# Layer 1 of a two-layer encoder: score units of a bank issued together, values with tokens on partitions for four heads, and splits on 128 rows laid out by DMA

## The chip, the cores and the metric

The kernel runs on one core of one Trainium2 chip. Its time is the device time of one execution in microseconds (us), and less is better. TensorE (PE) multiplies matrices out of SBUF into PSUM, VectorE (DVE), ScalarE (ACT) and GpSimd (POOL) work element by element, and SyncE (SP) issues most transfers. Each engine takes its instructions in order.

## The reference

A two-layer encoder over 512 tokens (an 8 x 64 grid) of width 1024, all in float32. Layer 0 has two head groups (grouped-query attention and latent attention) and is not touched but for one flag. Layer 1, which the change is about, is neighbourhood attention with 16 heads of 64:

```python
q, k, v = split(h @ w_qkv, 3)                       # 512 x 1024 each, 16 heads of 64
for each query: window of 8 rows x 16 columns       # all 8 rows of the grid, 16 columns
    sc = q . k[window] * 64**-0.5 + bias[head, row difference, column difference]
    o  = softmax(sc) . v[window]
h = h + o @ w_out
```

Each layer is followed by a squared-ReLU MLP of width 4096, and a final norm ends the whole.

## The kernel before

**Two halves of a number.** Every product is computed from numbers split into a high and a low part (`hi`, `lo`, a copy rounded by ScalarE and the rest by VectorE), as three matmuls: hi x hi, hi x lo, lo x hi. Lines 426 to 428 (`mm3`) are these three for the dense products, with the weights stationary and 512 tokens moving, so that outputs have their features on partitions. Weights come in chunks by `plan` and `weights` (two chunks ahead of their use, four `raw` buffers), are split into `whi` (L192, ScalarE) and `wlo` (L193, VectorE), and a product walks over its chunks.

**The attention of layer 1.** Tokens stand column by column of the grid (8 rows together), so that a block of 128 queries needs a band of 256 keys: a *unit*. A head has four units, u = 0 to 3, the last one for both ends of the sequence. For each unit, `unit` (L1207) issues two matmuls of 256 columns (L1217), which take the query's halves on the 128 rows of the contraction (64 features high, 64 low) against the key's high and low part. VectorE adds the bias and takes the minimum (L1221), ScalarE does the exponential (L1223), VectorE the reciprocal (L1224), GpSimd the normalisation (L1225). Two units share one PSUM bank `s` (there are two such banks): `scores` (L1228) calls `unit` for u = 3 and 0, then for 1 and 2, so the matmuls of a unit stand between the two halves' vector work in the program. The probabilities are transposed by TensorE (L1236, four 128 x 128 blocks for each of T1 and T2), split into halves (L1240 ScalarE, L1241 VectorE), and multiplied with the values in `finish` (eight matmuls, L1251), whose two halves are added (L1262, L1263).

**Projections.** `projC(t)` computes Q, K and V of the two heads 2t and 2t+1 at once: three column tiles of 128 in three `mm` banks, 8 k-tiles each, 72 matmuls of 512 columns. Its evacuation `ev` normalises (`hold["rb"]`, the reciprocal root of the norm, broadcast over partitions) and splits:

```python
                    for e in range(2):
                        a, z = 64 * e, 64 * (1 - e)
                        # Q: hi of head e on 64 rows, lo on the other 64     (L1177 ACT, L1178 DVE)
                        # K: hi and lo of head e on 64 rows, copied to the other 64
                        #                      (L1183 ACT, L1184 DVE, one DMA of GpSimd's queue, L1186)
```

So Q and K take two ScalarE and two VectorE instructions each, on 64 rows. V is normalised (L1189), transposed by TensorE in four blocks (L1192) to get tokens on partitions, and split (L1196, L1197).

**What sets the order.** The order of the instructions on each engine is fixed when the program is built, by a scheduler that takes the next instruction that its own timing has ready, in the order of the program otherwise. In the program, the attention of a head is written in three steps, and after each step `fill.run(us)` takes so many microseconds' worth of matmuls out of a queue of other products: first `projC(1)` to `projC(7)` (head 2t begins with `fill.until` of projection t), and from head 13 on the output projection of the first six head pairs. `projC(0)` runs ahead of the attention, with the sum of squares of the tokens (`rows_r1`: L446, a chain of small VectorE instructions, four transposes L454).

## Time and profile before

| what | value |
|---|---|
| runs shown | 1220.49, 1221.71, 1222.97 us; median 1221.71 |
| profiled execution | 1220.6 us, its span 1218.8 us |
| granted TensorE clock | 0.997 |
| TensorE matmuls busy | 1189.6 us (98%) |
| VectorE, ScalarE, GpSimd busy | 814.0, 628.3, 411.5 us |
| layer 1's projection ahead of the attention | begins at about 617 us |
| first and last score matmul of layer 1 | 641.3 and 840.6 us |

The span runs from the first to the last instruction that the profiler saw. A row of a group names line, engine, operation, output and inputs, shapes and count, then busy time and mean duration of one, then the idle time of the engine ahead of these instructions and what ended it. A row of the timeline gives the start, the duration (first start to last end where several are merged), and the instruction. A matmul's duration holds the way through the array, so matmuls of a stream overlap in their records.

### The profile page before, as it was taken

How to read it: one execution, taken by the hardware profiler on the slowest of the kernel's cores; microseconds unless marked ns; L12 is line 12 of the kernel's file. 1: busy time of each engine (PE TensorE's matmuls, PEld its weight loads, DVE VectorE, ACT ScalarE, POOL GpSimd, SP SyncE). 2: the span in 40 equal slices, each digit the busy share in tenths (PEclk: the TensorE clock that was granted, in tenths of full speed). 3: DMA queues.
4: the chain of work that ended last, by engine and by line, in shares of the span. 5: the costliest groups of instructions: out<-in, count | busy, mean ns of one | idle time of the engine just before them, and what ended most of it. 6: DMA issues, size and time to landing. Idle time of an engine off the chain costs nothing.

```text
span 1218.8 us, 18461 instructions
## 1 busy us (share of the span) xinstructions
PE 1189.6 (98%) x6644; PEld 1003.4 (82%) x6644; DVE 814.0 (67%) x1433; ACT 628.3 (52%) x1051; POOL 411.5 (34%) x535
## 2 busy tenths in 40 slices
PE   9998999999999999999999999999999999999997
PEld 8676788887899889898877777778788988988985
DVE  4587888878678338448566677675984763764764
ACT  5576676664446326235445565554563641451553
POOL 3256242205365146155001222111243913623700
PEclk9999999999999999999999999999999999999999
DMA  7223314212224224247224334323221341241332
GB/s 246 65 72 85 75 48 131 69 53 70 78 88 147 87 62 132 101 125 242 91 80 126 108 100 115 111 87 122 69 78 53 97 155 60 87 156 44 122 122 69
DMA packets 107259, 122.69 MB, mean 101 GB/s; under 512 B 8115, under 2 KB 81120, under 8 KB 107168
## 3 DMA queue, kind: packets, MB, share of 16 engines
q1 hardware_dynamic: 104880, 116.15, 30.9%
q0 software_dynamic: 1536, 4.21, 1.5%
q10 hardware_dynamic: 752, 1.15, 0.4%
q8 instruction: 52, 0.85, 0.3%
q14 instruction: 39, 0.32, 0.1%
HBM read 104.32 MB, written 6.29 MB: 91 GB/s over the span
## 4 chain that ended last, share of the span: by engine, by line
PE 78%; DVE 9%; ACT 4%; issue 3%; SPq 2%; POOL 2%; DMA 2%; DVEq 0%; POOLq 0%; ACTq 0%
PE mm L428 7%; PE mm L426 7%; PE mm L427 7%; PE s L428 2%; PE s L427 2%; PE s L426 2%; PE s L893 2%; PE o L873 2%; PE mm L316 2%; PE mm L314 2%; PE mm L315 2%; PE mm L1384 2%; PE mm L1383 2%; PE mm L1382 2%; PE t L860 2%
## 5 line engine op out<-in xcount | busy, mean ns | idle before, releaser
L193 DVE TENSOR_TENSOR wlo<-raw,whi 128x1024 fp32r<-128x1024 f32 (+2 forms) x141 | 158.7, 1127 | 152.7 <-ACT whi L192 149.5
L192 ACT ACTIVATE whi<-raw 128x1024 fp32r<-128x1024 f32 (+2 forms) x144 | 136.4, 949 | 168.0 <-PE o L427 38.7
L426 PE MATMUL mm<-a,whi 128*128 128x512 f32 x524 | 211.9, 406 | 0.4 <-DVE sc L790 0.4
L427 PE MATMUL mm<-a,whi 128*128 128x512 f32 x524 | 207.7, 396 | 0.1
L428 PE MATMUL mm<-a,wlo 128*128 128x512 f32 x524 | 207.2, 397 | 0.1
L240 DVE TENSOR_TENSOR wlo<-raw,whi 128x896 fp32r<-128x896 f32 x104 | 128.1, 1232 | 106.9 <-ACT whi L239 100.7
L239 ACT ACTIVATE whi<-raw 128x896 fp32r<-128x896 f32 x104 | 98.9, 951 | 161.5 <-PE s L1384 27.7
L234 POOL TENSOR_TENSOR raw<-raw 128x128 f32<-128x128 f32 x104 | 62.4, 600 | 271.5 <-DMA raw<-in_ffn_w_up_dram 204.7
L428 PEld LDWEIGHTS mm<-a,wlo 128*128 128x128 f32 x524 | 98.4, 188 | 23.2 <-issue 1.7
L427 PEld LDWEIGHTS mm<-a,whi 128*128 128x128 f32 x524 | 98.8, 189 | 20.2 <-issue 1.7
L426 PEld LDWEIGHTS mm<-a,whi 128*128 128x128 f32 x524 | 98.6, 188 | 20.3 <-issue 0.9
L236 POOL TENSOR_TENSOR raw<-raw 128x128 f32<-128x128 f32 x104 | 90.7, 872 | 8.1
L235 POOL TENSOR_TENSOR raw<-raw 128x256 f32<-128x256 f32 x104 | 87.9, 845 | 8.2
L1225 POOL TENSOR_SCALAR p<-p,ti 128x256 f32<-128x256 f32 x64 | 35.2, 556 | 134.4 <-DVE ti L1224 112.6
L316 PE MATMUL mm<-a,wlo 128*128 128x256 f32 x280 | 79.0, 282 | 1.6 <-DVE wlo L240 1.6
L315 PE MATMUL mm<-a,whi 128*128 128x256 f32 x280 | 78.6, 281 | 0.0
L314 PE MATMUL mm<-a,whi 128*128 128x256 f32 x280 | 78.6, 281 | 0.0
L901 POOL TENSOR_SCALAR p<-p,ti 128x512 f32<-128x512 f32 x64 | 46.6, 731 | 90.1 <-DVE ti L900 76.3
L316 PEld LDWEIGHTS mm<-a,wlo 128*128 128x128 f32 x280 | 52.8, 188 | 2.6 <-DVE wlo L240 2.6
L314 PE MATMUL t<-a,whi 128*128 128x256 f32 x192 | 53.9, 281 | 0.0
L315 PE MATMUL t<-a,whi 128*128 128x256 f32 x192 | 53.9, 281 | 0.0
L316 PE MATMUL t<-a,wlo 128*128 128x256 f32 x192 | 53.8, 280 | 0.0
(308 smaller groups left out, 3042.9 us busy)
## 6 DMA issues: line engine op xcount, KB each, us to landing
raw<-in_ffn_w_down_dram SPq DMA_DIRECT2D x64, 512.0 KB
raw<-in_ffn_w_up_dram SPq DMA_DIRECT2D x104, 256.0 KB
raw<-in_od_w_qkv_dram SPq DMA_DIRECT2D x64, 192.0 KB
raw<-in_ffn_w_up_dram SPq DMA_DIRECT2D x12, 512.0 KB
raw<-in_ev_w_in_dram SPq DMA_DIRECT2D x12, 384.0 KB
bias<-bx SPq DMA_DIRECT2D x16, 256.0 KB
a<-a POOLq DMA_DIRECT2D x16, 256.0 KB, 3.0
a<-a SPq DMA_DIRECT2D x10, 256.0 KB
```

Source lines behind the costliest of these rows:

```text
L192: ACT.activation(hi[:, 0:m], raw[:, 0:m], AF.Copy)
L193: (eng or DVE).tensor_tensor(lo_[:, 0:m], raw[:, 0:m], f32(hi[:, 0:m]), op=ALU.subtract)
L235: POOL.tensor_tensor(r[:, 4:6], r[:, 2:3].to_broadcast([P, 2, P]), r[:, 0:7:6], op=ALU.add)
L236: POOL.tensor_tensor(r[:, 7], r[:, 3], r[:, 5], op=ALU.subtract)
L239: ACT.activation(hi[:, 0:896], raw[:, 128:1024], AF.Copy)
L240: DVE.tensor_tensor(lo[:, 0:896], raw[:, 128:1024], f32(hi[:, 0:896]), op=ALU.subtract)
L314: PE.matmul(o, wh, x[:, 0], start=kp == 0 and z == 0, stop=False, skip_group_check=True)
L315: PE.matmul(o, wh, x[:, 1], start=False, stop=False, skip_group_check=True)
L316: PE.matmul(o, wl, x[:, 0], start=False, stop=kp == self.np - 1, skip_group_check=True)
L426: PE.matmul(o, wh, xh, start=first, stop=False)
L427: PE.matmul(o, wh, xl, start=False, stop=False)
L428: PE.matmul(o, wl, xh, start=False, stop=last)
```

## The change

1. **Scores.** `unit` keeps only the two matmuls; the vector work moves to a function `weigh`. `scores` first issues the matmuls of both units of a bank (only the first one starts the bank), then the vector work of both.
2. **Values.** `projC` computes Q and K alone (two column tiles, weights in chunks of four k-tiles). A new generator `valuesC(g)` computes V of four heads with the tokens stationary and 256 weight columns moving: 4 token blocks x 8 k-tiles x 3 = 96 matmuls of 256 columns, two token blocks in a bank. The result has tokens on partitions at once, so the transposes are gone; it is scaled by the per-token root `r1` and split in two pieces per bank. `valuesC(0)` runs first of all, in the `s` banks; `valuesC(1)` to `valuesC(3)` go into the queue behind `projC(2)`, `projC(4)` and `projC(6)`.
3. **Splits.** Q and K are split on all 128 rows by one ScalarE and one VectorE instruction. Three transfers of SyncE's queue put Q's halves in their places (the third overwrites what the first has read), three of GpSimd's queue K's.
4. **Rates and places.** `rows_r1` is called after 24 instead of 16 steps of the first product, and `fill.run` takes 3.4 for four heads instead of two.
5. **Layer 0.** In `v_part` both halves of a bank are computed before the first is evacuated, with one start of the bank.

```diff
@@ product
-                parts = [(0, ncols, src[:, :, :, runs[0][1] : runs[0][1] + runs[0][2]])]
+                parts = [(0, ncols, src[:, :, 0 : len(runs), runs[0][1] : runs[0][1] + runs[0][2]])]
@@ v_part (layer 0)
-                        PE.matmul(o, CK[k][:, 0, ts], wh, start=k == 0, stop=False, skip_group_check=True)
+                        PE.matmul(o, CK[k][:, 0, ts], wh, start=k == 0 and ii == 0, stop=False, skip_group_check=True)
...
-                    src = o.rearrange("p (h e) -> p h e", h=4)
+                for ii in range(2):
+                    i = 2 * ip + ii
+                    src = b[:, 256 * ii : 256 * ii + 256].rearrange("p (h e) -> p h e", h=4)
@@ projC, ev (the old splits and V's transposes are removed)
+            n_ = scratch()
+            if j == 0:
+                for to, fr, m in ((64, 0, 448), (0, 448, 64)):
+                    DVE.scalar_tensor_tensor(n_[:, to : to + m], b[:, fr : fr + m], 0.125,
+                                             hold["rb"][:, fr : fr + m], op0=ALU.mult, op1=ALU.mult)
+                d["Q"] = Slot()
+                q = d["Q"].pair()
+                lo = scratch(F32R)
+                ACT.activation(q[:, 0, :], n_, AF.Copy)
+                DVE.tensor_tensor(lo, n_, f32(q[:, 0, :]), op=ALU.subtract)
+                SP.dma_start(f32(q[0:64, 1, :]), f32(q[64:128, 0, :]))
+                SP.dma_start(f32(q[64:128, 1, :]), f32(lo[64:128, :]))
+                SP.dma_start(f32(q[64:128, 0, :]), f32(lo[0:64, :]))
             else:
+                DVE.tensor_tensor(n_, b, hold["rb"], op=ALU.mult)
+                d["K"] = [Slot(), Slot()]
+                ka, kb = (s_.pair() for s_ in d["K"])
+                split(n_, ka)
+                for z in range(2):
+                    POOL.dma_start(f32(kb[64 * z : 64 * z + 64, :, :]), f32(ka[64:128, :, :]))
+                POOL.dma_start(f32(ka[64:128, :, :]), f32(ka[0:64, :, :]))
-        return product(w_qkv, 0, XP, [(D * z + P * t, P) for z in range(3)], ev, three, stride=D)
+        return product(w_qkv, 0, XP, [(D * z + P * t, P) for z in range(2)], ev,
+                       lambda n: [mmb() for _ in range(n)], kstep=4, stride=D)
+    def valuesC(g, banks):
+        ids = [plan([(0, 256, rows(w_qkv, kk, 4)[:, :, 2 * D + 256 * g : 2 * D + 256 * g + 256])], 4, 256)
+               for kk in (0, 4)]
+        def run():
+            bk = banks()
+            VC[g] = []
+            def one(c, k, i):
+                hi, lo = (w[:, k, :] for w in weights(ids[c]))
+                o = bk[i // 2][:, 256 * (i % 2) : 256 * (i % 2) + 256]
+                x = XP[4 * c + k][:, :, i * P : (i + 1) * P]
+                first = c == 0 and k == 0 and i % 2 == 0
+                PE.matmul(o, x[:, 0], hi, start=first, stop=False, skip_group_check=True)
+                PE.matmul(o, x[:, 0], lo, start=False, stop=False, skip_group_check=True)
+                PE.matmul(o, x[:, 1], hi, start=False, stop=c == 1 and k == 3, skip_group_check=True)
+            for k in range(4):
+                for i in range(4):
+                    one(0, k, i)
+                    yield 0.355
+            for i in range(4):
+                for k in range(4):
+                    one(1, k, i)
+                    yield 0.355
+                if i % 2:
+                    VC[g].append(Slot())
+                    v = VC[g][-1].t.rearrange("p (i h e) -> p i h e", i=2, h=4)
+                    for ii in range(2):
+                        src = bk[i // 2][:, 256 * ii : 256 * ii + 256].rearrange("p (h e) -> p h e", h=4)
+                        r = hold["r1"][:, i - 1 + ii : i + ii]
+                        ACT.activation(v[:, ii, :, 0:64], src, AF.Copy, scale=r)
+                        DVE.scalar_tensor_tensor(v[:, ii, :, 64:128], src, r, f32(v[:, ii, :, 0:64]),
+                                                 op0=ALU.mult, op1=ALU.subtract)
+        return run()
@@ attend_C
             for n in range(2):
-                PE.matmul(s, lh, rh[n], start=n == 0, stop=n == 1, skip_group_check=True)
+                PE.matmul(s, lh, rh[n], start=first and n == 0, stop=n == 1, skip_group_check=True)
+        def weigh(h, u, s):
             ...
         def scores(h, us):
             sb = sbk()
             for n, u in enumerate(us):
-                h[u] = unit(h, u, sb[:, 256 * n : 256 * n + 256])
+                unit(h, u, sb[:, 256 * n : 256 * n + 256], n == 0)
+            for n, u in enumerate(us):
+                h[u] = weigh(h, u, sb[:, 256 * n : 256 * n + 256])
...
-                    PE.matmul(o[:, q0 : q0 + n], vv[:, kt, e, :], m.t[:, lo : lo + n],
+                    PE.matmul(o[:, q0 : q0 + n], vv[kt // 2][:, kt % 2, h["n"] % 4, :], m.t[:, lo : lo + n],
@@ start of the attention
-    gen = projC(0)
-    for n, _ in enumerate(gen):
+    first = valuesC(0, lambda: [sbk(), sbk()])
+    second = projC(0)
+    for n, _ in enumerate(first):
         ...
-        if n == 15:
+        if n == 23:
             rows_r1()
+    for _ in second:
+        pass
     for t in range(1, 8):
         fill.add(f"c{t}", projC(t))
+        if t in (2, 4, 6):
+            fill.add(f"c{t}", valuesC(t // 2, lambda: [mmb(), mmb()]))
@@ step
-        fill.run(3.4 if n < 2 else 2.85 if n < 13 else 4.0)
+        fill.run(3.4 if n < 4 else 2.85 if n < 13 else 4.0)
```

More of the change, by code (lines that the diff above doesn't have):

```diff
@@ new lines, in projC @@
+        return product(w_qkv, 0, XP, [(D * z + P * t, P) for z in range(2)], ev,
+                       lambda n: [mmb() for _ in range(n)], kstep=4, stride=D)
+    VC = {}
+    def valuesC(g, banks):
[13 more added lines that the diff above has]
+            for k in range(4):
+                for i in range(4):
+                    one(0, k, i)
[14 more added lines that the diff above has]
+        return run()
@@ L1203, in attend_C, with unit @@
     def attend_C(step):
         late = [None]
-        def unit(h, u, s):
+        def unit(h, u, s, first):
             d, e = h["d"], h["e"]
@@ L1245, in finish @@
             d, e = h["d"], h["e"]
-            vv = d["V"].t.rearrange("p (i h e) -> p i h e", i=4, h=2)
+            vv = [s_.t.rearrange("p (i h e) -> p i h e", i=2, h=4) for s_ in VC[h["n"] // 4]]
             o = ob()
@@ L1257, in finish @@
                 hold["pair"] = scratch()
-            else:
-                d["V"].free()
+            elif h["n"] % 4 == 3:
+                for s_ in VC[h["n"] // 4]:
+                    s_.free()
             c = scratch()
@@ L1279, in attend_C @@
                 fill.until(f"c{t}")
-            h = dict(d=PC[t], e=e)
+            h = dict(d=PC[t], e=e, n=n)
             h["bias"] = scp.tile([P, 2, 256], F32, tag="bias", bufs=2, name=nm("bias"))
```

33 lines of the change are left out of this document (removed).

## The prediction

> **What bounds the kernel now.** I read the page first, then the windows of the stage that the change touches, then the groups, waits and timeline of that stage.
>
> ```profile
> PE 1189.6 (98%) x6644; PEld 1003.4 (82%) x6644; DVE 814.0 (67%) x1433; ACT 628.3 (52%) x1051; POOL 411.5 (34%) x535
> PE 78%; DVE 9%; ACT 4%; issue 3%; SPq 2%; POOL 2%; DMA 2%; DVEq 0%; POOLq 0%; ACTq 0%
> core 0: us, PE busy (x) PEld busy (x) DVE busy (x) ACT busy (x) POOL busy (x), PEclk, DMA share, GB/s
> 640.60:842.00 201.40, 194.37 (x1008) 157.09 (x1007) 137.70 (x347) 114.33 (x249) 41.76 (x76) 1.00 0.38 108
> ```
>
> TensorE sets the end: it is busy for 98% of the span and carries 78% of the chain of waits. So an edit is worth the TensorE time it takes away, whether work or holes; on the other engines only what delays TensorE counts. From 640.6 to 842.0 us (the 16 heads of layer 1, without the tail) no other engine is near its limit: VectorE is busy for 137.7 of 201.4 us.
>
> Busy time hides holes here, because a matmul's record holds its pipeline tail. The pace is read from start to start in the timeline:
>
> ```profile
> 339.75 0.28 PE L315 MATMUL mm<-a,whi 128*128 128x256 f32 x1
> ...
> 342.93 0.28 PE L315 MATMUL mm<-a,whi 128*128 128x256 f32 x1
> ...
> 633.28 0.40 PE L426 MATMUL mm<-a,whi 128*128 128x512 f32 x1
> ...
> 638.18 0.39 PE L426 MATMUL mm<-a,whi 128*128 128x512 f32 x1
> ...
> 704.35 1.06 PE L1251 MATMUL o<-a,a 128*128 128x256 f32 x8
> 705.25 0.42 PE L1217 MATMUL s<-a,a 128*128 128x256 f32 x2
> ...
> 709.34 0.60 PE L1192 MATMUL t<-cst,sc 128*128 128x128 f32 x4
> 709.69 0.48 PE L426 MATMUL mm<-a,whi 128*128 128x512 f32 x1
> 710.00 0.39 PE L427 MATMUL mm<-a,whi 128*128 128x512 f32 x1
> ```
>
> Between the two rows of 512 columns lie 21 steps without a hole: 4.90 / 21 = 0.233 us each. Between those of 256 columns lie 27: 3.18 / 27 = 0.118. Eight of the values' matmuls take 0.90 (704.35 to 705.25), and four transposes 0.43 (709.34 to 710.00 less one 0.233), so 0.107 each. What the stage holds:
>
> ```profile
> L426 PE MATMUL mm<-a,whi 128*128 128x512 f32 x203 | 82.9, 408 | 0.0
> L428 PE MATMUL mm<-a,wlo 128*128 128x512 f32 x205 | 81.1, 396 | 0.0
> L427 PE MATMUL mm<-a,whi 128*128 128x512 f32 x204 | 80.7, 396 | 0.0
> L1217 PE MATMUL s<-a,a 128*128 128x256 f32 x128 | 28.7, 307 | 4.2 <-DVE ti L1221 4.0
> L1236 PE MATMUL t<-cst,p 128*128 128x128 f32 x120 | 19.0, 274 | 1.0 <-POOL p L1225 1.0
> L1251 PE MATMUL o<-a,a 128*128 128x256 f32 x60 | 12.3, 286 | 0.0
> L1251 PE MATMUL o<-a,a 128*128 128x192 f32 x60 | 11.0, 265 | 0.0
> L1192 PE MATMUL t<-cst,sc 128*128 128x128 f32 x28 | 4.5, 282 | 1.8 <-DVE sc L1189 1.7
> ```
>
> 612 x 0.233 = 142.6, 128 x 0.118 = 15.1, 148 transposes x 0.107 = 15.8, 15 sets of eight x 0.90 = 13.5: 187.0 of 201.4 us. So about 14 us are holes, and the idle column says where: at the scores (L1217) for VectorE, and at the transposes of the values (L1192).
>
> **The second score unit of a bank.** Two units share a bank. In the kernel before, the second unit's first matmul starts a new sum in the bank in which VectorE still reads the first unit.
>
> ```profile
>   DVE ti L1221: 17.7, 38
> ...
> 707.14 0.40 PE L427 MATMUL mm<-a,whi 128*128 128x512 f32 x1
> 708.52 0.51 PE L1217 MATMUL s<-a,a 128*128 128x256 f32 x2 [0.98 <-DVE ti L1221]
> 708.87 0.40 PE L428 MATMUL mm<-a,wlo 128*128 128x512 f32 x1
> ...
> 840.10 0.40 PE L428 MATMUL mm<-a,wlo 128*128 128x512 f32 x1
> 840.34 0.49 PE L1217 MATMUL s<-a,a 128*128 128x256 f32 x2
> 840.67 0.40 PE L426 MATMUL mm<-a,whi 128*128 128x512 f32 x1
> ```
>
> Line L1217 waited 38 times for VectorE's reading (17.7 us with the weight loads' idle time, 4.0 us of the matmuls alone). A long wait: 708.52 - 707.14 - 0.233 = 1.15 lost, and the pair takes 0.35 instead of 0.236: 1.26 in all, 0.28 more than the 0.98 shown idle. A short one (840.34) still lengthens its pair to 0.33, 0.10 lost, with no idle time shown. The waits of the whole stage count seven long ones with 4.0 us: 4.0 + 7 x 0.28 = 6.0. The other 31 at 0.10 to 0.19 give 3.1 to 6. I take 4.5: 10.5 us in sum. In the changed order all four score matmuls of a bank stand together with no wait among them, so **-10.5**, before what comes back.
>
> The Trainium skill, "PSUM — Partial Sum Buffer", "PSUM bank collisions raise a hardware error", says that accesses of one bank are to be guarded by bank and quadrant, not by address. The waits of L1217 on the other half of its bank agree. By that rule, dropping the flag alone would not free the second unit; putting all four matmuls ahead of the first reading does.
>
> **What comes back at the probability transposes (L1236).** In the changed order, twelve fill matmuls (12 x 0.233 = 2.8 us) stand between the scores of units 1 and 2 and the transposes, as many as before; the transpose that needs unit 1 comes after three others. So unit 1's probabilities must be there 0.47 + 2.8 + 0.32 = 3.6 us after the scores begin. The hole that TensorE spent at the second unit used to be part of this cover and is gone.
>
> ```profile
> L1225 POOL TENSOR_SCALAR p<-p,ti 128x256 f32<-128x256 f32 x62 | 34.3, 559 | 128.7 <-DVE ti L1224 106.8 <-PE mm L428 13.3 <-PE mm L427 7.7
> L1223 ACT ACTIVATE p<-p,ti 128x256 f32<-128x256 f32 x64 | 32.3, 504 | 16.0 <-DVE ti L1221 14.9
> L1221 DVE CUSTOM_DVE_ANT_0 p<-s,bias 128x256 f32<-128x256 f32 x64 | 27.0, 422 | 24.1 <-PE s L1217 16.9 <-issue 3.6 <-PE t L1236 2.3
> ...
> 704.58 1.40 DVE L1178 TENSOR_TENSOR a<-sc,a 64x512 fp32r<-64x512 f32 x2
> 706.01 1.40 DVE L1184 TENSOR_TENSOR a<-sc,a 64x512 fp32r<-64x512 f32 x2
> 707.44 0.68 DVE L1263 TENSOR_TENSOR sc<-o,sc 64x512 f32<-64x512 f32 x1
> 708.05 0.41 DVE L1221 CUSTOM_DVE_ANT_0 p<-s,bias 128x256 f32<-128x256 f32 x1
> ```
>
> The chain is: end of the four matmuls 0.64 (the last starts at 0.36 and lasts 0.28 like the rows of 256 columns); VectorE 0.42; exponential 0.50 and its sum 0.2; VectorE again, behind unit 2's 0.42 and the 0.68 of L1263; GpSimd 0.56; handovers of about 0.1 each: 3.2 to 3.6 us. That just fits when VectorE is free. When it isn't, as at 704.58 to 708.05, where Q's and K's splits and L1263 held unit 1's reading for 2.4 us after its scores, TensorE waits for the whole delay. The change thins this: Q's and K's splits lose two of four VectorE instructions (2 x 0.70 us per head pair), their two halves are now evacuated 2.8 us apart, and the values' evacuation moves elsewhere; but weight splits come in larger pieces. Bounds: 1 us over all heads if every chain fits, 9 us if the delays of before (1.2 to 2.4 us in five of 16 heads, smaller ones in others) stand in full. I take **+4.0**, nearer the low end, since the 3.5 us bursts fall apart.
>
> **Values with tokens on partitions.** Removed: 8 k-tiles x 3 x 8 head pairs = 192 matmuls x 0.233 = 44.7 us, and 32 transposes x 0.107 = 3.4. Added: 4 x 96 = 384 matmuls of 256 columns x 0.118 = 45.3. Work: **-2.8**. The weight loads double per column, but L314 to L316 also load new weights for every 256 columns and keep 0.118. The waits ahead of the transposes go too: three with 1.7 us idle plus 0.28 each, and about six short ones at 0.1: **-3.1**. Nothing on TensorE follows the new evacuation at once: the values are needed at L1251, two steps after a head's scores.
>
> The Trainium skill, "TensorE: Matmul & The Clock Gate", "Part 4: PE-mode transpose", gives some 275 ns for one transpose. The records agree (274 ns), the pace doesn't: by 275 ns the 32 would have cost 8.8 us, and the work term would be -8.2. The start-to-start rows decide.
>
> **Splits on 128 rows.** ScalarE and VectorE halve their instructions for Q and K; neither is the bound, so nothing directly. Laid out by DMA: three SyncE transfers per Q, the third after the first has landed, and three GpSimd ones per K, the third after both others. Ahead of the first head this is on the path:
>
> ```profile
> a<-a POOLq DMA_DIRECT2D x16, 256.0 KB, 3.0
> DMA to landing us min/median/max: 2.8/3.0/5.4
> ```
>
> (The second row is of the K copies' line, L1186.) K: two VectorE and one ScalarE step of 0.6 to 0.7 each (L1263's and L1178's rows), perhaps one weight split of the same pace per column, 1.2 to 1.4, between them, then 0.56 for a second issue and two landings of 3.0 one behind the other: about 10 us. In the built order 50 fill matmuls (11.7 us) stand between the last matmul of the first K and the first score, so it is covered, by 1.7 us; with slow landings (5.4) it is not. Later head pairs have their K and Q at least one head's fill (8 us or more) ahead. On SyncE, weight and bias loads queue behind Q's transfers, which wait for VectorE; weights are asked for two chunks ahead, of 24 x 0.233 = 5.6 us each, which hides a landing of 3 us. On GpSimd, the third copy holds the normalisation behind it only if the first two haven't landed.
> The start also changes: values come first, and the norm's reciprocal root has 20 matmuls of 0.118 = 2.4 us of cover instead of 14 x 0.233 = 3.3. Both together: bounds 0 and 4, taken **+1.5**.
>
> **The end of the fill.** Projections left for the attention shrink from 7 x 72 x 0.233 = 117 to 7 x 48 x 0.233 + 3 x 96 x 0.118 = 112 us, while four instead of two heads now draw 3.4 per step. So the queue runs dry in head 12, about two steps before the output projection is added, and TensorE meets bare chains of 3 us there, partly filled by the next head's scores. Bounds 0 and 3, taken **+1.5**.
>
> Layer 0's values (L816) get the same flag: four places, at most 0.5 us; I take 0.
>
> **Sum.** -10.5 + 4.0 - 2.8 - 3.1 + 1.5 + 1.5 = -9.4. The profiled execution took 1220.6 us (span 1218.8), so 1211.2; the median of the runs is 1.1 above it: **1212.3 us**. With all bounds at their good end it is -17 (1205), with all at their bad end +1 (1223).
>
> **Rivals.** *The wait only moves*: the holes of L1217 reappear at L1236 in full (+9), the start and the dry spell cost 2.5 each: -2.4, so 1219. For it: TensorE passes from 12 matmuls straight to a chain of the same length. Against: the VectorE bursts are split.
> *GpSimd is held (slower)*: the third K copy waits on GpSimd for two landings, and the normalisations queued behind it stop. It decides from the point where the copies are issued less than 3 us before a head's exponentials; at 2 us or more for each of seven head pairs this gives +14 on the -9.4, so about 1226. For it: GpSimd works in order, and landings took up to 5.4. Against: in the built order the third copy mostly stands a pair of normalisations later.
> *Nothing comes back* (the chains fit everywhere, start and end are covered): 1206.
> That the change doesn't do what it says is ruled out by the order: no wait stands inside the four score matmuls.
>
> **How the numbers follow.** Forecast 0.62, the wait only moves 0.18, GpSimd held 0.12, nothing comes back 0.08. The range 1205 to 1220 takes in the forecast with its bounds, the last rival and most of the first; it leaves out the slower case and the far corner in which all bounds are bad at once. About 0.2% (2.4 us) is what a measurement can tell: faster = 0.62 + 0.08 + half of 0.18 = 0.79, same 0.09, slower 0.12.
>
> **What would show it.** Right: the score line waits for VectorE (almost) nowhere; the stage from the first to the last score is shorter by its holes; no transposes of values; waits of the transposes for GpSimd rise from 1.0 to some 3 us. Wrong: over 8 us of waits at the transposes; scores waiting for K's copies beyond the first head; GpSimd waiting for a DMA with TensorE behind it.

## The result, and the profile after

The changed kernel takes **1211.66 us** (median of four runs, 1210.92 to 1212.64) against 1221.74 (four runs too, 1220.49 to 1222.97): a ratio of 0.9911, 95% interval 0.9892 to 0.993. (The two medians alone give 0.9918, well inside the interval.) The forecast was 1212.3. The profiled execution took 1211.92 us with a span of 1210.0, which is 8.8 less than the 1218.8 of before.

The page of the changed kernel, engines and chain:

```profile
PE 1182.8 (98%) x6804; PEld 1012.4 (84%) x6804; DVE 797.6 (66%) x1409; ACT 615.0 (51%) x1035; POOL 424.5 (35%) x543
PE 81%; DVE 8%; ACT 3%; POOL 3%; issue 2%; DMA 1%; SPq 1%; DVEq 0%; POOLq 0%; ACTq 0%
```

TensorE still sets the end, and more of the chain is its own (81% for 78%). The heads of layer 1, from the first score to the last matmul of the values: the window (columns as in the prediction) and the groups of TensorE in it that answer to those of before. L1248 is the score line (L1217 before), L1271 the transposes of the probabilities (L1236), L1208 to L1210 the new values.

```profile
652.60:839.00 186.40, 182.22 (x1109) 159.18 (x1110) 119.69 (x325) 101.14 (x233) 48.32 (x85) 1.00 0.48 131
```

```profile
L1208 PE MATMUL mm<-whi,a 128*128 128x256 f32 x96 | 27.7, 289 | 0.0
L1248 PE MATMUL s<-a,a 128*128 128x256 f32 x128 | 21.1, 287 | 1.9 <-ACT a L742 1.6 <-DMA a<-a 0.3
L1271 PE MATMUL t<-cst,p 128*128 128x128 f32 x128 | 20.9, 275 | 3.4 <-POOL p L1258 3.4
```

Three things are to be seen. The scores wait for VectorE nowhere (4.0 us of such idle time before). The transposes wait 3.4 us for GpSimd's normalised probabilities (1.0 before). And no transposes of values are left. The 1.6 us that the scores still wait stand at one place, the very first head. The row names ScalarE's L742 for it, but that is the split of the next pair's K, which these scores do not read; in the trace the last copy of the first K lands at 652.54 us, and the first score starts at 652.63.

Idle time alone is not the loss. From here on a *hole* is the time from one matmul's start to the next less the pace of the rows in the prediction (0.233 us for 512 columns, 0.118 for 256; 0.109 for a transpose), summed by the line that starts late. Over the heads this gives 14.5 us of holes before and 6.5 after. The hole ahead of the very first score is not in these sums: 1.75 us in the changed kernel, none in the kernel before.

### The profile page after: what moved, and what is told of

It reads as the page before. It is cut to its first block, busy times and chain, and to the rows that moved or that the text cites. A ratio compares the mean times of both kernels' runs of the same rounds, so it can differ in the third digit from the quotient of the medians.

```text
span 1210.0 us, 18784 instructions
## 1 busy us (share of the span) xinstructions
PE 1182.8 (98%) x6804; PEld 1012.4 (84%) x6804; DVE 797.6 (66%) x1409; ACT 615.0 (51%) x1035; POOL 424.5 (35%) x543
## 4 chain that ended last, share of the span: by engine, by line
PE 81%; DVE 8%; ACT 3%; POOL 3%; issue 2%; DMA 1%; SPq 1%; DVEq 0%; POOLq 0%; ACTq 0%
PE mm L428 7%; PE mm L427 7%; PE mm L426 7%; PE s L428 2%; PE s L426 2%; PE s L427 2%; PE o L875 2%; PE s L895 2%; PE mm L316 2%; PE mm L314 2%; PE mm L315 2%; PE mm L1424 2%; PE mm L1425 2%; PE mm L1423 2%; PE t L862 2%
## 5 line engine op out<-in xcount | busy, mean ns | idle before, releaser
L193 DVE TENSOR_TENSOR wlo<-raw,whi 128x1024 fp32r<-128x1024 f32 (+2 forms) x133 | 157.4, 1185 | 156.5 <-ACT whi L192 153.3
L426 PE MATMUL mm<-a,whi 128*128 128x512 f32 x460 | 185.6, 406 | 0.1
L427 PE MATMUL mm<-a,whi 128*128 128x512 f32 x460 | 183.1, 398 | 0.1
L428 PE MATMUL mm<-a,wlo 128*128 128x512 f32 x460 | 182.0, 397 | 0.1
L428 PEld LDWEIGHTS mm<-a,wlo 128*128 128x128 f32 x460 | 86.6, 189 | 21.1 <-issue 1.7
L427 PEld LDWEIGHTS mm<-a,whi 128*128 128x128 f32 x460 | 87.1, 189 | 18.9 <-issue 1.7
L426 PEld LDWEIGHTS mm<-a,whi 128*128 128x128 f32 x460 | 86.8, 189 | 18.4 <-issue 1.0
L235 POOL TENSOR_TENSOR raw<-raw 128x256 f32<-128x256 f32 x104 | 95.3, 917 | 8.2
L316 PE MATMUL mm<-a,wlo 128*128 128x256 f32 x280 | 79.3, 283 | 1.8 <-DVE wlo L240 1.6
L314 PE MATMUL mm<-a,whi 128*128 128x256 f32 x280 | 78.6, 281 | 0.0
L316 PEld LDWEIGHTS mm<-a,wlo 128*128 128x128 f32 x280 | 52.7, 188 | 3.0 <-DVE wlo L240 2.8
L314 PE MATMUL t<-a,whi 128*128 128x256 f32 x192 | 53.9, 281 | 0.0
L316 PE MATMUL t<-a,wlo 128*128 128x256 f32 x192 | 53.8, 280 | 0.0
```

What stands on the lines that cost most here:

```text
L193: (eng or DVE).tensor_tensor(lo_[:, 0:m], raw[:, 0:m], f32(hi[:, 0:m]), op=ALU.subtract)
L235: POOL.tensor_tensor(r[:, 4:6], r[:, 2:3].to_broadcast([P, 2, P]), r[:, 0:7:6], op=ALU.add)
L314: PE.matmul(o, wh, x[:, 0], start=kp == 0 and z == 0, stop=False, skip_group_check=True)
L316: PE.matmul(o, wl, x[:, 0], start=False, stop=kp == self.np - 1, skip_group_check=True)
L426: PE.matmul(o, wh, xh, start=first, stop=False)
L427: PE.matmul(o, wh, xl, start=False, stop=False)
```

## The experiments

Twelve kernels; every median is of five or more executions, except four in the runs named e3_splits, e7_cover, e9_cover_k and e10_more_cover. The kernel before took 1221.48, 1221.9 and 1222.71 us beside the three groups (e1 to e4, e5 to e8, e9 to e12). The hole ahead of the first score comes on top of the last column: 1.0 us in e2_values and e5_scores_values, 1.2 in e3_splits, 2.9 in e6_splits_lead, 1.9 in e7_cover, 0.9, 0.9 and 0.7 in e8 to e10, none in the others.

| kernel | median, us | ratio to before, 95% interval | holes in the heads, us (first score left out) |
|---|---|---|---|
| before / changed | 1221.74 / 1211.66 | 0.9911, 0.9892 to 0.993 | 14.5 / 6.5 |
| e1_scores | 1215.91 | 0.9958, 0.9946 to 0.9971 | 9.4 |
| e2_values | 1222.76 | 1.001, 1.0001 to 1.0019 | 16.1 |
| e3_splits | 1235.34 | 1.0113, 1.0098 to 1.0128 | 30.0 |
| e4_vpart | 1218.68 | 0.9978, 0.9968 to 0.9988 | 14.5 |
| e5_scores_values | 1214.53 | 0.9941, 0.9927 to 0.9954 | 7.4 |
| e6_splits_lead | 1217.38 | 0.9963, 0.995 to 0.9975 | 8.9 |
| e7_cover | 1207.15 | 0.988, 0.9864 to 0.9896 | 4.5 |
| e8_first_k | 1210.25 | 0.9908, 0.9893 to 0.9922 | 8.8 |
| e9_cover_k | 1206.33 | 0.9867, 0.9853 to 0.988 | 3.4 |
| e10_more_cover | 1207.02 | 0.9869, 0.9856 to 0.9883 | 2.3 |
| e11_lead | 1217.57 | 0.9962, 0.9949 to 0.9975 | 10.8 |
| e12_flag_kept | 1219.37 | 0.9976, 0.9966 to 0.9986 | 14.4 |

### One part alone: the joined scores

```diff
-                PE.matmul(s, lh, rh[n], start=n == 0, stop=n == 1, skip_group_check=True)
+                PE.matmul(s, lh, rh[n], start=first and n == 0, stop=n == 1, skip_group_check=True)
+        def weigh(h, u, s):
...
             for n, u in enumerate(us):
-                h[u] = unit(h, u, sb[:, 256 * n : 256 * n + 256])
+                unit(h, u, sb[:, 256 * n : 256 * n + 256], n == 0)
+            for n, u in enumerate(us):
+                h[u] = weigh(h, u, sb[:, 256 * n : 256 * n + 256])
```

> The kernel before with one part of the change alone: all four score matmuls of a bank stand together, under one start flag, ahead of the first reading. Values with tokens on columns, splits on 64 rows and layer 0 stay as before. My theory: the holes at the second unit (10.5 us) go and some 3 to 4 us come back at the probability transposes, so -6 to -7.5 us, about 1215. Rival 'the wait only moves': the transposes take over nearly all of it, -2 us or less, about 1220. Rival 'nothing comes back': -10.5, about 1211. In the profile: the score line waits for VectorE nowhere; the transposes' wait for GpSimd is about 3 us (mine), about 9 us (the wait only moves) or about 1 us (nothing comes back).

1215.91 us, so -5.1 in the ratio: a little under my range. The groups of the heads (636 to 850 us) in this kernel:

```profile
L1217 PE MATMUL s<-a,a 128*128 128x256 f32 x128 | 20.6, 284 | 0.0
L1240 PE MATMUL t<-cst,p 128*128 128x128 f32 x128 | 20.5, 276 | 0.9 <-POOL p L1227 0.9
L1192 PE MATMUL t<-cst,sc 128*128 128x128 f32 x32 | 5.3, 287 | 5.2 <-DVE sc L1189 5.0
```

The scores wait for nothing, as forecast, and the probability transposes wait no longer than before (0.9). But the wait came back somewhere else: at the value transposes, which this kernel still has, from 1.7 to 5.0 us (their holes from 2.7 to 6.7). TensorE now meets VectorE's late evacuations there. Neither theory had named that place.

### One part alone: the values with tokens on partitions

The edit takes `valuesC` with its calls, the projection of Q and K in two columns and the fill's amounts from the changed kernel; the scores stay unit by unit and the splits on 64 rows.

```diff
-        return product(w_qkv, 0, XP, [(D * z + P * t, P) for z in range(3)], ev, three, stride=D)
+        return product(w_qkv, 0, XP, [(D * z + P * t, P) for z in range(2)], ev,
+                       lambda n: [mmb() for _ in range(n)], kstep=4, stride=D)
+    def valuesC(g, banks):
...
```

> The kernel before with the values alone changed: tokens on partitions for four heads at a time, ahead of Q and K at the start, with the projections of Q and K in two columns and the fill's amounts of the changed kernel. Scores unit by unit and splits on 64 rows as before. My theory: less work 2.8 us and no waits ahead of the value transposes 3.1 us, and almost nothing back at the dry end of the fill (+0.3): about -5.6, 1216. Rival 'work only': the waits reappear at the second unit's matmuls, because VectorE's evacuations still meet there: -2.8, 1219. Rival 'by the record's duration of a transpose': 32 x 0.275 instead of 32 x 0.107 saved: -11, 1211.

1222.76 us: no gain at all, a ratio of 1.001. My -5.6 fell; the rival "work only" had the right mechanism, and it went further than it said, and not only at the second unit.

```profile
L1246 PE MATMUL s<-a,a 128*128 128x256 f32 x128 | 28.9, 307 | 6.5 <-DVE ti L1250 5.4 <-DMA a<-a 0.8
L1265 PE MATMUL t<-cst,p 128*128 128x128 f32 x128 | 21.0, 275 | 2.9 <-POOL p L1254 2.8
```

The value transposes are gone with their wait of 1.7 us, and the second unit's matmuls and the probability transposes wait 1.4 us longer for VectorE and 1.8 longer for GpSimd. The first score has a hole of 1.0 us besides, where it waits for K's copy (0.8 us idle in its row).

### Both together

The changed kernel without two of its parts, the splits and layer 0's values:

```diff
-                split(n_, ka)
-                for z in range(2):
-                    POOL.dma_start(f32(kb[64 * z : 64 * z + 64, :, :]), f32(ka[64:128, :, :]))
...
+                for e in range(2):      # as before: 64 rows at a time, one copy each
...
-                        PE.matmul(o, CK[k][:, 0, ts], wh, start=k == 0 and ii == 0, stop=False, skip_group_check=True)
+                        PE.matmul(o, CK[k][:, 0, ts], wh, start=k == 0, stop=False, skip_group_check=True)
```

> The changed kernel without two of its parts: splits of Q and K on 64 rows, and layer 0's values, as before; so the joined scores and the values with tokens on partitions together. Alone they gave -5.1 and +1.2 us by the medians (of 1221.48). Additive: -4, 1217.5. My theory: alone each one's wait found another customer of VectorE's late evacuations (the value transposes, then the second unit); together only the probability transposes are left, so more than the sum: holes of the attention about 8 us (14.5 before) and 2.7 us less work, -8, about 1213.5. Rival 'the wait only moves': the probability transposes take over what both had, holes of 14 us, and only the work is saved, -2.7, 1218.8.

1214.53 us: -7.2 by the ratio, where -5.1 and +1.2 (by their ratios) add up to -3.9. My theory held.

```profile
L1269 PE MATMUL t<-cst,p 128*128 128x128 f32 x128 | 21.5, 276 | 4.6 <-POOL p L1256 4.4
L1246 PE MATMUL s<-a,a 128*128 128x256 f32 x128 | 20.8, 285 | 0.8 <-DMA a<-a 0.8
```

Of three places where TensorE could meet a late VectorE (second unit, value transposes, probability transposes) one is left. The joined scores are worth 5.1 us on the kernel before and 8.2 on top of the values (1222.76 to 1214.53): what a removed wait is worth depends on whether another line stands ready to take it over.

### One part alone: the splits on 128 rows

Shown is K's part of the edit; Q's goes the same way over SyncE's queue.

```diff
-                for e in range(2):
...
-                        POOL.dma_start(f32(kt[z : z + 64, :, :]), f32(kt[a : a + 64, :, :]))
+                    split(n_, ka)
+                    for z in range(2):
+                        POOL.dma_start(f32(kb[64 * z : 64 * z + 64, :, :]), f32(ka[64:128, :, :]))
+                    POOL.dma_start(f32(ka[64:128, :, :]), f32(ka[0:64, :, :]))
```

> The kernel before with the splits of Q and K alone changed: on 128 rows, laid out by three SyncE and three GpSimd transfers per head pair. Values, scores and layer 0 as before. My theory: only the relay of K's copies ahead of the first head is on the path, about +1.8 us (0 to 4), 1223.5. Rival 'the relief of VectorE counts': its bursts ahead of the second unit's reading lose two of four instructions of 0.7 us per head pair, so the score line's wait for VectorE (4.0 us) halves: -2 to -4 net, 1218 to 1220. Rival 'GpSimd is held': the third K copy stops the normalisations behind it, which shows as more than 4 us of waits of the transposes for GpSimd: +4 or more, over 1225.

1235.34 us, 1.1% slower: the size of my rival "GpSimd is held", but not its mechanism. The profiled execution took 1239.88, 4.5 us more than the median, so its holes are on the large side. First the groups, then the timeline ahead of one head pair (L743 ends K's split, L1185 and L1186 issue the copies):

```profile
L1217 PE MATMUL s<-a,a 128*128 128x256 f32 x120 | 28.8, 327 | 15.9 <-issue 13.3 <-DVE ti L1221 1.5 <-DMA a<-a 1.1
L1236 PE MATMUL t<-cst,p 128*128 128x128 f32 x116 | 18.7, 275 | 0.4 <-POOL p L1225 0.4
```

```profile
794.60 0.67 DVE L1180 TENSOR_TENSOR sc<-mm,rb 128x512 f32<-128x512 f32 x1
...
796.01 0.69 DVE L743 TENSOR_TENSOR a<-sc,a 128x512 fp32r<-128x512 f32 x1
797.00 1.07 POOL L1185 DMA_DIRECT2D a<-a  x2 [1.01 <-DVE a L743]
...
803.92 0.56 POOL L1186 DMA_DIRECT2D a<-a  x1 [2.79 <-DMA a<-a]
808.19 0.48 PE L1217 MATMUL s<-a,a 128*128 128x256 f32 x2 [3.12 <-issue]
```

The transposes wait 0.4 us for GpSimd, less than before, so GpSimd holds nobody. The scores themselves wait for the copies: 6.9 us from the issue of two copies to that of the third, which needs both landed, and 4.3 more to the score. "Issue" in the idle column names no releaser; the timeline supplies it. In the built order K's last matmul stands 7.2 to 11.7 us of matmuls ahead of the first score of pairs 0 to 6 in the kernel before, 11.7 to 13.9 here, and 11.9, 14.0 and then 17 to 26 in the changed kernel. Cover plus hole is 12.6 to 15.8 us at these seven pairs here. The relay takes that long. The changed kernel has that much from the third pair on; its projections of Q and K come without the values' third column, and four heads instead of two draw 3.4 us of fill. Which of the two gives the cover was not tested apart, but the next runs show that more fill alone does.

### The same with a lead, and the lead alone

```diff
-        fill.run(3.4 if n < 2 else 2.85 if n < 13 else 4.0)
+        fill.run(4.2 if n < 4 else 2.85 if n < 13 else 4.0)
```

> The kernel before with the splits on 128 rows alone, as in the run that took +13.9 us, and 4.2 instead of 3.4 (head 0 and 1) or 2.85 (2 and 3) us of fill per step in the first four heads, so that a projection of Q and K is done about 8 to 16 us ahead of its first head instead of 4. Theory 'the relay needs a lead': the holes at the first scores of head pairs (1 to 3.6 us each in the run without the lead) go from the third pair on and shrink at the second; what is left is the relay ahead of the first pair and a drier end: +1 to +4 against before, 1222.5 to 1225.5. Rival 'GpSimd's copies themselves disturb' (the third copy holds GpSimd 27 us in sum, and transfers compete with weights): the holes stay, 1233 or more.

> The kernel before with the fill's lead alone: 4.2 us per step in the first four heads, splits on 64 rows as before. The splits on 128 rows with this lead gave -4.5 us, without it +13.9. Theory 'the relief of VectorE pays, once the relay is covered': the lead alone gives little, -1 (0 to -2), 1220.5, and the other 3.5 us are the splits'. Rival 'the lead pays': projections done early take VectorE's evacuations away from the scores and value transposes; alone it gives -4 or more, 1217.5, and the splits themselves nothing.

With the lead the loss of the splits is gone: 1217.38 us, more than I had expected, since the kernel before gains as much from the lead alone (1217.57; ratios 0.9963 and 0.9962). So in sum the splits give nothing. The traces show two parts that cancel: the value transposes' holes go from 3.0 us in e11_lead to none in e6_splits_lead, which looks like a relief of VectorE, and in their place the relay of the first pair, which the lead does not reach, costs 2.9 us ahead of the first score (the first row, of e6_splits_lead). The other two rows are of the lead alone:

```profile
PE s L1217 <- issue: 2.7, 1, 2.7
```

```profile
L1217 PE MATMUL s<-a,a 128*128 128x256 f32 x128 | 28.2, 304 | 0.8 <-DVE ti L1221 0.7
L1192 PE MATMUL t<-cst,sc 128*128 128x128 f32 x32 | 5.2, 286 | 1.8 <-DVE sc L1189 1.6
```

With all instructions as before, the second unit's wait for VectorE fell from 4.0 to 0.7 us (its holes from 10.6 to 6.5): what has moved is where the evacuations stand against the scores. The profiled execution of e11_lead was its slowest, 1221.05 us: its heads end 3.0 us earlier than in the kernel before, and the part behind them takes 3.4 us longer, with the clock at half for 6.8 us at the start of the second MLP (last section). So the gain of the lead is shown by the five times, and only its place by the trace. Whether that would hold for another lead was not tried; e2_values has a lead too and its scores wait longer.

### Layer 0: order or flag

```diff
-                        PE.matmul(o, CK[k][:, 0, ts], wh, start=k == 0, stop=False, skip_group_check=True)
+                        PE.matmul(o, CK[k][:, 0, ts], wh, start=k == 0 and ii == 0, stop=False, skip_group_check=True)
...
-                    src = o.rearrange("p (h e) -> p h e", h=4)
+                for ii in range(2):
+                    i = 2 * ip + ii
+                    src = b[:, 256 * ii : 256 * ii + 256].rearrange("p (h e) -> p h e", h=4)
```

e4_vpart is this edit alone; e12_flag_kept is its second half, with the start flag as before.

> The kernel before with layer 0's values alone changed: one start flag for both halves of a bank, and their evacuation after both. Layer 1 as before. I had forecast 0 (at most 0.5 us), 1221.5. The changed kernel reached layer 0's MLP 2.7 us earlier than the one before. Theory 'the flag pays there': -2.7, 1219. Rival 'the new order of the evacuations shifts the engines of layer 0 by chance' also gives -2.7 here, but no wait of the values line is behind it; the two are told apart by which line's waits go: the values' matmuls (the flag) or others. If neither, the 2.7 us must come from layer 1's plan reaching back, and this kernel stays at 1221.5.

> The kernel before with layer 0's evacuation of the values moved behind both halves, but the start flag kept at each half; the built order of all engines is that of the run that changed both (1218.7). Theory 'the order of the evacuation pays': the same -2.8, 1218.7. Rival 'the flag pays' (the second half's new sum waited for the first half's reading): no gain, 1221.5, or a wait at the values' matmuls.

Ratios 0.9978 and 0.9976: the 2.7 us are real, and the flag has no part in them. The values' line waited for nobody in the kernel before either (its row, idle 0.0). Below that row stand two waits of the kernel before in layer 0 that neither of these two kernels has:

```profile
L816 PE MATMUL mm<-whi,a 128*128 128x256 f32 x16 | 4.6, 287 | 0.0
```

```profile
PE t L860 <- POOL p L901: 0.9, 2, 0.8
PE mm L426 <- DVE sc L790: 0.4, 1, 0.4
```

In the built order the evacuations on ScalarE and VectorE stand elsewhere, and a head's reading of scores comes ahead of a weight split where it came behind. Holes of 0.25 to 0.93 us at seven places of layer 0's attention, 3.3 us in sum, are gone (one of 0.68 down to 0.24), and two of a quarter us are new: from 130 to 340 us the holes are 7.8 us in the kernel before, 5.1 in e4_vpart and 5.0 in e12_flag_kept. The largest, 0.93, stood behind a normalisation of GpSimd that took 1.20 instead of 0.69 us while VectorE computed the low half of a weight chunk (L193; see the last section); in the new order that one is gone. For the others the runs show no rule that makes this order the better one.

### Better versions: cover at the transposes, K of the first pairs

In the changed kernel the largest hole stands at head 4, unit 1 (timeline):

```profile
699.55 1.06 ACT L192 ACTIVATE whi<-raw 128x1024 fp32r<-128x1024 f32 x1 [0.36 <-PE mm L427]
...
700.51 0.62 ACT L742 ACTIVATE a<-sc 128x512 fp32r<-128x512 f32 x1
...
701.04 0.49 ACT L1256 ACTIVATE p<-p,ti 128x256 f32<-128x256 f32 x1
...
701.89 1.21 DVE L193 TENSOR_TENSOR wlo<-raw,whi 128x1024 fp32r<-128x1024 f32 x1
...
702.14 2.34 POOL L1258 TENSOR_SCALAR p<-p,ti 128x256 f32<-128x256 f32 x2 [4.71 <-DVE ti L1257]
...
703.08 0.68 DVE L743 TENSOR_TENSOR a<-sc,a 128x512 fp32r<-128x512 f32 x1
...
704.08 0.33 PE L1271 MATMUL t<-cst,p 128*128 128x128 f32 x1 [1.68 <-POOL p L1258]
```

A weight split and K's split stand on ScalarE ahead of the exponential. The first of the two normalisations then takes GpSimd from 702.14 to 704.02, four times the usual 0.48 us, while VectorE computes the low halves of a weight chunk (L193) and of K (L743). That is most of the hole; the last section comes back to it. So e7_cover deals the fill out otherwise, e8_first_k takes the long relay from the first pair, e9 does both (K of two pairs), e10 deals out more.

```diff
-        fill.run(3.4 if n < 4 else 2.85 if n < 13 else 4.0)
+        fill.run((3.4 if n < 4 else 2.85 if n < 13 else 4.0) + (-0.5, 0.9, -0.4)[z])
...
+                if t == 0:        # t < 2 in e9 and e10; (-0.8, 1.5, -0.7) in e10
+                    for e in range(2):
...
+                        POOL.dma_start(f32(kt[z : z + 64, :, :]), f32(kt[a : a + 64, :, :]))
+                    return
```

> The changed kernel with the fill of each head dealt out otherwise: 0.9 us more between the scores of units 1 and 2 and the transposes that need unit 1, 0.5 less ahead of the values' matmuls and 0.4 less after the transposes. Theory 'the chain of unit 1 is short of cover by a fixed time': of the 4.9 us of holes at the probability transposes 0.9 each goes in eight places, -3 to -4 us, about 1208. Rival 'the holes follow bursts of VectorE and ScalarE' that the fill itself brings: the bursts move with the fill, and the gain is under 1 us, 1211 to 1212. Rival 'the cover taken away is missed elsewhere': waits of the values' matmuls or of the scores for what now has 0.4 to 0.5 us less, 1212 to 1214.

1207.15 us. The wait of the transposes falls from 3.4 to 2.2 us, the holes of the heads by 2.0. That is half of the 4.5 us between the medians (the 95% intervals of the two kernels just touch, but each of its four times lies below each of the changed kernel's). In the profiled executions 2.4 us more stand at the start of the next MLP, where the clock fell in the changed kernel and not in this one (last section); that the dealing of the fill does this is not shown. So the fixed-time theory was too simple: the short holes of some 0.5 us mostly went, the two behind bursts stayed (1.4 and 0.9 us, 1.9 and 0.9 in the changed kernel).

> The changed kernel with the first head pair's K split on 64 rows and copied by two transfers side by side, as before; all else as in the changed kernel. Theory: the 1.75 us hole ahead of the first score is the second of K's two landings one behind the other and goes in full: -1.7 us, 1210. Rival: the weights' transfers and Q's relay land as late, and nothing changes (within 0.5 us, 1211.7). Rival: the two extra pairs of VectorE and ScalarE instructions delay the scores as much as the landing did: 0 or up to +1.

1210.25 us, within the measurement of the changed kernel. The hole ahead of the first score went from 1.75 to 0.9, but the first score then came earlier, and the second pair's K had 11.9 instead of 14.0 us of cover: its scores waited 2.5 us (0.3 before), and the clock fell behind them, as the row and the window (clock in the third column from the end) say:

```profile
667.63 0.71 PE L1257 MATMUL s<-a,a 128*128 128x256 f32 x4 [2.52 <-issue]
```

```profile
668.60:672.00 3.40, 3.40 (x13) 2.89 (x12) 2.28 (x9) 2.77 (x7) 0.47 (x1) 0.53 0.18 41
```

> The changed kernel with the fill dealt out as in the run with more cover (1207.15), and the K of the first two head pairs (not only of the first) split on 64 rows and copied side by side. From the built order, K's last matmul stands 11.9 and 14.0 us of matmuls ahead of the first score of pairs 0 and 1 in the changed kernel and 6.8 and 11.7 here; the holes of the earlier runs there say that the relay of three copies takes about 14.5 us from that matmul and the two copies side by side about 7.7. Theory: holes of about 0.9 at the first score and none at the second pair's, against 1.9 and 0.0 with the cover alone and 0.9 and 2.7 with one K of the old kind alone: -1 us on the cover alone, about 1206. Rival: VectorE's and ScalarE's extra instructions take it back, 1207 to 1208.

> As the run before it, with 1.5 instead of 0.9 us moved between the scores of units 1 and 2 and the transposes that need unit 1 (0.8 and 0.7 less at the two other places). Theory 'short of cover by a fixed time': the 1.4 and 0.9 us holes that stood at two heads shrink by 0.6 each, -1 us, 1205. Rival 'taken from the wrong place': the values' matmuls or the next scores now wait, +1, 1207.

1206.33 and 1207.02 us, ratios 0.9867 and 0.9869. With two pairs on the short way the scores wait 0.8 us in all:

```profile
L1257 PE MATMUL s<-a,a 128*128 128x256 f32 x128 | 20.7, 285 | 0.8 <-ACT whi L192 0.8
L1280 PE MATMUL t<-cst,p 128*128 128x128 f32 x128 | 20.4, 274 | 2.0 <-POOL p L1267 1.9
```

Both beat the changed kernel (the intervals do not touch); against the cover alone they overlap. The further cover lowers the holes from 3.4 to 2.3 us, but the time does not show it.

## Why the prediction was right, point by point

The time was right because the largest terms were, and, by luck, because the errors of the others cancelled: +1.8 (work), +0.8 (start), +2.5 (the MLP behind) and 0.9 of small ones against -1.0 (come-back), -1.5 (end of the fill) and -2.7 (layer 0).

- **The second unit, -10.5.** Measured -10.2: holes at the score line of 10.6 us before, 0.4 after when the copies' waits are left out. Right. The two readings that made it, long waits with 0.28 lost beyond the idle time and short ones with no idle time at all, are needed: the idle column alone says 4.0.
- **What comes back at the transposes, +4.0.** Measured +3.0 (1.9 to 4.9 us of holes). Right in place and nearly in size, and bursts of VectorE are behind it as reckoned, with ScalarE's beside them. One link of the chain was not: the sum has 0.56 us for a normalisation, and four of the five holes over 0.25 us stand behind one that took 0.77 to 1.88 (last section). The rival "the wait only moves" held for e2_values, where what the value transposes lost came back in full; in e1_scores 4.0 of the 10.2 us came back, and at a place that it did not name.
- **The value transposes' waits, -3.1.** Measured 3.1 us of holes gone.
- **The values' work, -2.8.** About -1.0: by the paces alone -2.8, but the 384 new matmuls ran at 0.121 instead of 0.118 us in the mean (1.2), and each of the eight sets of transposes had given the next matmul 0.08 us back, which goes with it (0.6). By the Trainium skill's 275 ns for one transpose ("TensorE: Matmul & The Clock Gate", "Part 4: PE-mode transpose") it would have been -8.2; the trace of after lies on the side of the pace.
- **The start, +1.5.** +2.3: 1.75 us ahead of the first head, 0.5 at the second pair. I had put the relay at 10 us with a cover of 11.7. It took over 13, as the timeline of the changed kernel shows (L1181 reads K's bank, L743 ends the split, L1186 and L1187 copy):

```profile
639.45 0.69 DVE L1181 TENSOR_TENSOR sc<-mm,rb 128x512 f32<-128x512 f32 x1 [0.65 <-PE mm L428]
...
641.51 0.68 DVE L743 TENSOR_TENSOR a<-sc,a 128x512 fp32r<-128x512 f32 x1
641.61 7.49 SPq L183 DMA_DIRECT2D raw<-in_od_w_qkv_dram  x8
642.78 1.16 POOL L1186 DMA_DIRECT2D a<-a  x2 [77.43 <-DVE a L743]
...
648.71 0.51 POOL L1187 DMA_DIRECT2D a<-a  x1 [4.77 <-DMA a<-a]
...
652.63 0.59 PE L1248 MATMUL s<-a,a 128*128 128x256 f32 x3 [1.58 <-ACT a L742]
```

  The landing of the first two was mis-sized: 5.9 us from the issue instead of 3.6 (0.56 + 3.0), with eight weight transfers asked for in the same time. So this step failed: the relay was not covered, and at the second pair the scores waited for K's copies too, which the prediction had named as a sign of being wrong, if only 0.5 us. That the pairs from the third on were covered was right, but not for my reason ("8 us or more" is less than the relay): they have 17 to 26. With 12 the kernel would presumably have been slower, as e3_splits was. The point from which the slower rival decides was the right question, asked of the wrong engine.
- **The end of the fill, +1.5.** Mis-sized: no hole above 0.4 us stands in heads 12 to 15. The drying queue cost nothing that shows.
- **GpSimd held.** It does wait, 21.9 us in sum, and almost nobody waits for it: who waited for the first two copies of a K (L1186), and who for the third (L1187):

```profile
  POOL a L1187: 21.9, 7
```

```profile
  PEld s L1248: 0.8, 1
  PE s L1248: 0.3, 1
```

- **Layer 0, 0.** Missed: -2.7 (e4_vpart). I had priced the flag, and the edit also moves two evacuations in a planned order.
- **The MLP behind, not named.** +2.5 in the profiled execution, mostly the clock (below).

Summed, the layer's terms give -10.2 + 3.0 - 3.1 - 1.0 + 2.3 = -9.0, and the matmuls L314 to L316 of the MLP ahead of the heads had 0.6 more of holes: -8.4, beside -8.4 measured from layer 0's MLP to the last matmul of the heads. With -2.7 and +2.5 the span's -8.8 is reached to 0.2.

What gave the gain by runs: the joined scores and the values 7.2 together and layer 0's order 2.7, by the ratios; 9.9 of 10.9, with an interval of some 2.3 us on either side (by the medians 7.4 + 2.8 = 10.2 of 10.1). So nothing clear of the noise is left for the splits. The changed kernel has no value transposes that they could relieve.

## What to carry to other kernels

Before a removed wait is booked as a gain, list the lines of the bounding engine that meet the same late producer: in a pipeline with several such lines the wait goes to the next one, and parts that give -5.1 and +1.2 alone gave -7.2 together. A layout step by DMA is priced by the matmuls that the built order puts between its producer and its first reader; count them for each head pair, and change the dealing of the fill before the copies. In a planned order an edit that seems free can move others: price the new order, not the edit. And list the sparse stretches of TensorE: here every step of 3.4 us filled to 0.43 or less was followed by 3.4 us at half clock.

## What the runs showed of the hardware

The clock of TensorE fell to half for 3.4 us after short holes. First the changed kernel, start of the second MLP: the stretch ahead, with a hole of 1.66 us, and the one behind. Then e7_cover at the same place, behind a hole of 1.67, with no fall. Then e3_splits behind a hole of 3.4 us (clock in the third column from the end).

```profile
856.00:859.90 3.90, 2.31 (x14) 1.83 (x13) 3.90 (x6) 0.00 (x0) 0.00 (x0) 0.99 0.01 3
859.90:863.30 3.40, 3.40 (x10) 2.65 (x9) 2.88 (x14) 0.00 (x0) 0.00 (x0) 0.51 0.90 279
```

```profile
855.30:858.70 3.40, 3.40 (x15) 2.76 (x16) 3.09 (x9) 0.00 (x0) 0.00 (x0) 1.00 0.60 183
```

```profile
808.50:811.90 3.40, 3.40 (x12) 2.73 (x11) 1.77 (x7) 1.77 (x5) 0.47 (x1) 0.53 0.02 5
```

Eight matmuls of 512 columns ran at 0.42 instead of 0.233 us in the changed kernel: 1.5 us lost that no wait shows. In e3_splits 37 matmuls of 192 to 512 columns were slowed so, in four places, and 5.0 us of its loss are not holes of waiting but what followed them. The Trainium skill ("TensorE: Matmul & The Clock Gate", "What's actually happening") has the clock at half after an idle window of some 3.4 us, the window running freely. The half and the 3.4 us agree, and a free window would explain that the same hole costs 1.5 us in one kernel and nothing in another; but 1.7 us of hole in a sparse stretch was enough here.

The traces bear the free window out and put a number to "sparse". In each trace the falls start on one grid of 3.413 us: in e3_splits at 699.48, 726.79, 781.40 and 808.71 us, which are 8, 16 and 8 steps apart, in the changed kernel at 115.74 and 859.85, 217 steps apart. Cut each of the 14 traces into the steps of its own grid, from 130 us to 12 us ahead of the end, leave out the steps at half clock, and add up the paces of the matmuls in each step. Twelve steps are filled to 0.43 or less, and each of them is followed by a fall; the other 4376 are filled to 0.46 or more, and none is. In the changed kernel the hole and the few small matmuls behind it fall into one step, filled to 0.32; in e7_cover they are divided between two, the emptier filled to 0.51. So a hole can cost about twice its length, and whether it does depends on where the grid lies. The grid does not lie at the same place in all of these traces; how often each kernel is hit is not shown, since one execution of each was traced.

The second thing is GpSimd's normalisation (128x256), which takes 0.48 us and at times much longer. In the changed kernel 10 of 64 take 0.77 to 2.05 us. All ten run beside VectorE's subtractions L193 or L743, which read two operands of SBUF, for 0.42 us or more; none of the other 54 does for over 0.29. In the kernel before it is 9 of 64 (0.68 or more, against 0.34 at most), in e7_cover 9 (0.42, against 0.33). In e9_cover_k one of the usual length lies wholly beside such a subtraction, so running side by side does not decide it alone. The holes at the transposes at 657, 704, 751 and 774 us of the changed kernel each stand right behind such a long normalisation. No run moves the subtractions alone, so this is read off the traces and not tested.
